# Second block of a two-block transformer kernel: GpSimd's arithmetic moved to VectorE, output projection in plain fp32, modulation sums moved

## The chip, the cores and the metric

The kernel runs on one core of a Trainium2 chip. TensorE (PE in the rows; PEld is its loading of weights), VectorE (DVE), ScalarE (ACT), GpSimd (POOL) and SyncE (SP, which only issues DMAs here) each work through their own list of instructions in order, and wait for each other by semaphores. The metric is the device time of one execution in microseconds (us), lower is better.

## The reference

The reference is two transformer blocks over 256 tokens of width 1024, in fp32. The first has attention (8 heads with a sliding window, 8 with forget gates) and a gated feed-forward part. The second block is what the change touches:

```python
mod = silu(c) @ w_ada + b_ada
sh_a, sc_a, g_a, sh_f, sc_f, g_f = split(mod, 6)
h = rmsnorm(x) * (1 + sc_a) + sh_a
qa, ka, va, q_lat, kv_lat, k_rope = split(h @ w_in)
o_a = windowed_gqa(qa, ka, va, sink)            # 8 heads, rotary, window 128
o_b = latent_attention(q_lat, kv_lat, k_rope)   # 8 heads, up-projections w_q_up, w_kv_up
mixed = concat([rmsnorm(o_a, g1), rmsnorm(o_b, g2)])
x = x + g_a * (mixed @ w_out)
h = rmsnorm(x) * (1 + sc_f) + sh_f
x = x + g_f * peer(h)                           # 16384 experts, 8 heads x 16 picks
```

It ends with a last norm of the rows. `peer` computes queries and scores, picks 16 experts a head, and in this kernel multiplies with all the rows of the two expert tables, `u` and `v`, 64 MB each.

## The kernel before

Tokens lie on the 128 partitions, in two tiles. A product in fp32 accuracy is made of three products of the type fp32r: both operands are split into a high part (a copy in fp32r) and a low part (the rest), and `mm3` (lines 141 to 145) adds high times high, high times low and low times high into one bank of PSUM. The operands of the two tiles of tokens stand split in `xh` and `xl`.

Weights come as units of 128 rows by up to 1024 columns. `plan` lists the units in the order of their use, `fetch` starts some, `unit` hands the next one out. `load` (lines 106 to 116) does three things for a unit: a DMA from SP's queue into one of three buffers `x`, a copy by ScalarE into one of four buffers `hi` (line 114), and a subtraction into one of four buffers `lo` (line 115). That subtraction is VectorE's work, but for the units that the list `POOLED` (line 38) names: all of `w_out_2` (output projection of the second block), seven of the eight of `w_swa` (its input projection for the windowed attention), `w_kvup` and both of `w_qup`. For those it is GpSimd's.

The stages around the change, in their order of time:

- The end of the feed-forward part (`ffn`, lines 960 to 1005): norms of two tiles of rows, the step to the operands of the second block (`scaled` transposes, `shifted` multiplies and adds, `split` makes `xh` and `xl`), and the products `lat_proj` with the weights `w_lat`. The low parts of the first tile's operands are GpSimd's work (line 604), those of the second VectorE's. VectorE and ScalarE keep the written order here (`in_order`).
- The input projection `swa_proj`, eight units with 12 products each, then `swa_rope`, which rotates queries and keys on VectorE (lines 1031 to 1036), `kv_up` and `q_up(0)`.
- The attention (`steps`, `attend`): eight pairs of heads, four of windowed attention (`swa`) and four of latent attention (`mla`). A pair goes through its stages one step behind the other: scores (line 410), maximum (414, 417 and 420), exponentials on ScalarE (427), division (447), transposes (465), product with the values (480), and the split of the outcome, times a gain, into `oh` and `ol` (491 and 494). A table of fills gives each step other work of TensorE, among it the output projection `wo`: pairs 0 and 1 in step 7, 2 and 3 in step 8, 4 in step 9.
- The tail (lines 1222 to 1257): products of pairs 5, 6 and 7, in TensorE's written order; `row_scale(sqb)`, the norm of the latent half; `post`, which scales a half of a tile, adds it to the rows (lines 536 and 537) and sums their squares; then the norm, the transposes and the operands of `peer`, whose query products come next. Two of the four additions of `post` and the first tile's low parts are GpSimd's.
- `ada_cols` makes 16 small products (line 229) that sum two of the six modulation vectors: 16 columns of them for shift 3 in step 1, for scale 4 in the tail.

Outside the stretches that `in_order` holds, a scheduler orders the instructions of each engine by the dependences of the written program.

## Time and profile before

| | |
|---|---|
| median of 3 runs | 1306.51 us (1304.98 to 1307.62) |
| the profiled execution, first to last instruction | 1306.6 us |
| TensorE busy | 1269.4 us, 97% |
| VectorE busy | 970.5 us, 74% |
| ScalarE busy | 684.5 us, 52% |
| GpSimd busy | 86.8 us, 7% |
| subtractions of weights on GpSimd (line 115) | 23, 50.9 us |
| share of the chain that ended last | PE 90%, DVE 7%, ACT 2%, DMA 1% |

The busy time of TensorE counts pipelined products whose ends are modelled, so the rate of a run of products is read from their starts. The granted clock (PEclk) is given as a share of 2.4 GHz: 1.00 is that level, 0.50 is 1.2 GHz, what lies between is a mixture over the stretch. GpSimd's share of the span is small, but nearly all of it lies between 318 and 464 us, the stretch from the end of the feed-forward part to the first query products of `peer`.

### The profile page before, as it was taken

What the parts mean: (1) busy time and instruction counts of PE and PEld (TensorE: products, weight loads), DVE (VectorE), ACT (ScalarE), POOL (GpSimd) and SP (SyncE); (2) the same over time, 40 slices, a digit from 0 to 9 for tenths busy, and PEclk for the clock granted to TensorE, in tenths of its full rate; (3) what the DMA queues carried; (4) which work ended last, traced back from release to release, by engine and by line L of the source; (5) the groups of instructions that cost most, each with busy time, mean ns of one, the idle gap of its engine ahead of it and who ended that gap; (6) DMA issues with size and microseconds to landing.
All of it is one profiled execution on the core that took longest, in us unless ns stands there. A gap on an engine that the chain in (4) does not pass through costs nothing.

```text
span 1306.6 us, 22860 instructions
## 1 busy us (share of the span) xinstructions
PE 1269.4 (97%) x8804; PEld 1160.8 (89%) x8804; DVE 970.5 (74%) x1908; ACT 684.5 (52%) x1241; POOL 86.8 (7%) x70
## 2 busy tenths in 40 slices
PE   8999999999888899999999999999999999999997
PEld 7887899999766699999999999999988888888886
DVE  5678878877777879989777889997555855555555
ACT  6655544454567455456555554445444554444543
POOL 2300100000351400000000000000000000000001
PEclk9999999999998989999999999999999999999999
DMA  6756588886241355555444444444576855555552
GB/s 216 217 188 216 184 289 292 285 281 226 62 135 31 116 191 169 186 169 192 158 135 146 146 145 145 139 149 167 186 253 208 296 195 186 193 177 193 190 185 93
DMA packets 67849, 239.50 MB, mean 183 GB/s; under 512 B 8499, under 2 KB 9155, under 8 KB 67452
## 3 DMA queue, kind: packets, MB, share of 16 engines
q1 hardware_dynamic: 66524, 233.53, 52.9%
q0 software_dynamic: 1216, 4.51, 1.1%
q8 instruction: 69, 1.13, 0.3%
q14 instruction: 40, 0.33, 0.1%
HBM read 235.87 MB, written 2.79 MB: 183 GB/s over the span
## 4 chain that ended last, share of the span: by engine, by line
PE 90%; DVE 7%; ACT 2%; DMA 1%; issue 1%; ACTq 0%; DVEq 0%
PE ps L143 24%; PE ps L144 23%; PE ps L145 23%; PE ps L345 3%; PE ps L348 3%; PE ps L347 3%; PE ps L1459 2%; PE ps L1460 2%; PE ps L410 1%; PE ps L465 1%; PE ps L480 1%; DVE lo L115 1%; PE ps L1486 1%; PE ps L229 0%; DVE h L537 0%
## 5 line engine op out<-in xcount | busy, mean ns | idle before, releaser
L114 ACT ACTIVATE hi<-x 128x1024 fp32r<-128x1024 f32 (+2 forms) x384 | 403.2, 1052 | 433.2 <-PE ps L145 181.6
L115 DVE TENSOR_TENSOR lo<-x,hi 128x1024 fp32r<-128x1024 f32 (+2 forms) x361 | 439.0, 1218 | 201.2 <-ACT hi L114 196.6
L143 PE MATMUL ps<-xh,hi 128*128 128x256 f32 (+2 forms) x1304 | 378.2, 290 | 1.4 <-ACT xh L573 1.0
L144 PE MATMUL ps<-xl,hi 128*128 128x256 f32 (+2 forms) x1304 | 368.5, 283 | 1.5 <-DVE xl L574 1.5
L145 PE MATMUL ps<-xh,lo 128*128 128x256 f32 (+2 forms) x1304 | 368.6, 283 | 0.0
L143 PEld LDWEIGHTS ps<-xh,hi 128*128 128x128 f32 (+1 forms) x1304 | 247.3, 190 | 3.2 <-ACT xh L573 1.2
L144 PEld LDWEIGHTS ps<-xl,hi 128*128 128x128 f32 (+1 forms) x1304 | 247.3, 190 | 2.7 <-POOL lo L115 1.7
L145 PEld LDWEIGHTS ps<-xh,lo 128*128 128x128 f32 (+1 forms) x1304 | 246.3, 189 | 0.6
L144 PE MATMUL ps<-lo,w 128*128 128x512 f32 (+1 forms) x640 | 223.3, 349 | 0.0
L143 PE MATMUL ps<-hi,w 128*128 128x512 f32 (+1 forms) x640 | 223.2, 349 | 0.0
L145 PE MATMUL ps<-hi,w 128*128 128x512 f32 (+1 forms) x640 | 221.9, 347 | 0.0
L143 PEld LDWEIGHTS ps<-hi,w 128*128 128x128 f32 x640 | 121.2, 189 | 16.9 <-ACT hi L114 0.2
L145 PEld LDWEIGHTS ps<-hi,w 128*128 128x128 f32 x640 | 120.8, 189 | 16.0
L144 PEld LDWEIGHTS ps<-lo,w 128*128 128x128 f32 x640 | 121.2, 189 | 15.4 <-issue 0.2
L345 PE MATMUL ps<-xh,hi 128*128 128x256 f32 x352 | 100.0, 285 | 0.6 <-ACT xh L573 0.6
L348 PE MATMUL ps<-xh,lo 128*128 128x256 f32 x352 | 98.7, 281 | 0.0
L347 PE MATMUL ps<-xl,hi 128*128 128x256 f32 x344 | 96.5, 281 | 0.0
L1469 DVE SCALAR_TENSOR_TENSOR W<-ps,W 128x160 f32<-128x160 f32 (+31 forms) x64 | 55.1, 865 | 31.0 <-ACT W L1508 30.2
L115 POOL TENSOR_TENSOR lo<-x,hi 128x1024 fp32r<-128x1024 f32 (+1 forms) x23 | 50.9, 2222 | 323.3 <-ACT hi L114 323.3
L345 PEld LDWEIGHTS ps<-xh,hi 128*128 128x128 f32 x352 | 66.2, 188 | 1.6 <-ACT xh L573 0.9
L348 PEld LDWEIGHTS ps<-xh,lo 128*128 128x128 f32 x352 | 66.3, 188 | 0.0
L347 PEld LDWEIGHTS ps<-xl,hi 128*128 128x128 f32 x344 | 65.1, 189 | 0.7
(346 smaller groups left out, 1706.2 us busy)
## 6 DMA issues: line engine op xcount, KB each, us to landing
x<-in_u SPq DMA_DIRECT2D x128, 512.0 KB, 3.5
x<-in_v SPq DMA_DIRECT2D x128, 512.0 KB, 3.5
x<-in_w_gu SPq DMA_DIRECT2D x44, 512.0 KB, 4.6
ada<-in_w_ada SPq DMA_DIRECT2D x40, 512.0 KB, 5.0
x<-in_w_down SPq DMA_DIRECT2D x22, 512.0 KB, 4.5
x<-in_w_in SPq DMA_DIRECT2D x18, 512.0 KB, 4.4
x<-in_w_out SPq DMA_DIRECT2D x16, 512.0 KB, 3.4
x<-in_w_query SPq DMA_DIRECT2D x16, 512.0 KB, 3.7
```

The lines of the kernel that those rows point to most:

```text
L114: nc.scalar.activation(hi[:, :w], x[:, :w], AF.Copy)
L115: low.tensor_sub(lo[:, :w], x[:, :w], hi[:, :w].bitcast(F32))
L143: mm(out, lhsT=lh, rhs=rh, start=start, stop=False)
L144: mm(out, lhsT=lh, rhs=rl, start=False, stop=False)
L145: mm(out, lhsT=ll, rhs=rh, start=False, stop=stop)
L345: mm(out, lhsT=wh[:, s], rhs=self.xh[:, k, :T], start=k == 0, stop=False)
L347: mm(out, lhsT=wh[:, s], rhs=self.xl[:, k, :T], start=False, stop=False)
L348: mm(out, lhsT=wl[:, s], rhs=self.xh[:, k, :T], start=False, stop=not apart and k == KT - 1)
L410: nc.tensor.matmul(S[tl, hd], lhsT=qT(tl, hd), rhs=kT(hd, n), start=True, stop=True)
L1459: nc.tensor.matmul(o, lhsT=bj[:, gq, :, q], rhs=ah[:, gq, :, q], start=True, stop=False)
L1460: nc.tensor.matmul(o, lhsT=bj[:, gq, :, q], rhs=al[:, gq, :, q], start=False, stop=True)
L1469: nc.vector.scalar_tensor_tensor(a, pv[:, :, :i0], 1.0 / GSC, a, op0=OP.mult, op1=OP.mult)
```

## The change

No arithmetic is left on GpSimd from the end of the feed-forward part to the end of the tail; it keeps one DMA there, which stores the rows. `POOLED` is gone, so the low parts of all split units are made by VectorE. The units of `w_out_2` are no longer split: `whole` loads them by DMA straight into rooms of the `hi` and `lo` buffers, by turns, as fp32. The outcome of a pair of heads is kept as one fp32 tile `o` instead of `oh` and `ol`, and `plain` multiplies it with the unit in fp32: four products for a pair, where there were twelve.

```diff
+WHOLE = ("w_out_2",)
-POOLED = [("w_out_2", c) for c in (0, 1, 2, 3, 4, 5, 6, 7)] + [("w_swa", c) for c in (0, 1, 2, 4, 5, 6, 7)] + [("w_kvup", None), ("w_qup", 0), ("w_qup", 1)]
...
+    def whole(self, name, i, w):
+        self.rooms = not self.rooms
+        n, b = (("lo", self.nl), ("hi", self.nh))[self.rooms]
+        x = self.strm.tile([128, 1024], F32R, name=self.nm("x"), tag=n, bufs=b).bitcast(F32)
+        self.nc.sync.dma_start(x[:, :w], self.t[name][i * 128:(i + 1) * 128])
+        return x
...
-        oh = w.tile([128, T], F32R, name=self.nm("oh"), tag="oh", bufs=6)
-        ol = w.tile([128, T], F32R, name=self.nm("ol"), tag="ol", bufs=6)
...
+            oh, ol = w.tile([128, T], F32, name=self.nm("o"), tag="o", bufs=8), None
             nc.scalar.activation(oh, O[:, :T], AF.Copy, scale=g)
...
-            nc.vector.scalar_tensor_tensor(ol, O[:, :T], g, oh.bitcast(F32), op0=OP.mult, op1=OP.subtract)
...
+    def plain(self, acc, c, o, w, start, stop, tiles=(0, 1)):
+        for tt in tiles:
+            for hf in range(2):
+                self.nc.tensor.matmul(acc[tt][hf], lhsT=o[:, tt * 128:(tt + 1) * 128], rhs=w[:, hf * 512:(hf + 1) * 512],
+                                      start=start, stop=stop)
```

In `ffn` the low parts of the first tile's operands go to VectorE, put off to a later place in its list, and the first three units of `w_swa` are fetched there, ahead of the second tile's operands (`plan` and `fetch` used to follow after `lat_proj`):

```diff
-            self.split(ym[0], 0, 0, (nc.gpsimd, nc.vector)[BX])
+            low = []
+            self.split(ym[0], 0, 0, nc.vector, low)
...
+            run(low)
             self.sum2(sr[:, 3:4], s2[1])
-            r = self.rstd(sr[:, 3:4], 1, D, lambda: self.split(ym[0], 0, 1, nc.gpsimd))
+            r = self.rstd(sr[:, 3:4], 1, D, lambda: self.split(ym[0], 0, 1, nc.vector, low))
             lat_proj(0, range(4))
             p1 = [self.scaled(xn[1], r, 1, hf) for hf in range(2)]
+            run(low)
             lat_proj(0, range(4, 8))
+            self.plan(*(("w_swa", i, 768) for i in range(8)))
+            self.fetch(3)
```

In the second block the sums for shift 3 move ahead of the attention, those for scale 4 from the tail into step 1. All eight units of `w_out_2` are fetched before the attention's first step, behind two units of `w_query`. Pairs 5 and 6 of the projection move from the tail into steps 9 and 10. In the tail the products of pair 7 for the second tile stand behind `row_scale`, and the four additions of `post` are VectorE's:

```diff
+        self.ada_cols(16, 3)
         swa_T(4)
         swa_T(0)
+        self.fetch(sum(s[0] == "w_out_2" for s in self.todo))
...
-            1: [do(swa_T, 2), do(self.ada_cols, 16, 3)] + ([do(q_up, 1)] if QL == 2 else []),
+            1: [do(swa_T, 2), do(self.ada_cols, 24, 4)] + ([do(q_up, 1)] if QL == 2 else []),
...
-            9: [fin, do(wo, 4)],
+            9: [fin, do(wo, 4), do(wo, 5)],
+            10: [do(wo, 6), lambda: self.fetch(2)],
...
-            for hf in range(2):
-                self.part(acc[4], items[:2], 0, hf)
+            self.plain(acc[4], 7, outs[7][0], last, False, True, (0,))
             rg = row_scale(sqb)
-            for part in (items[2:], 0), (items, 1):
-                for hf in range(2):
-                    self.part(acc[4], part[0], part[1], hf)
-            self.ada_cols(24, 4, late)
-            post(0, 0, nc.gpsimd)
-            post(0, 1)
-            post(1, 0, nc.gpsimd)
-            post(1, 1)
+            self.plain(acc[4], 7, outs[7][0], last, False, True, (1,))
+            for tt in range(2):
+                for hf in range(2):
+                    post(tt, hf)
...
-                self.split(ym[0], 0, hf, nc.gpsimd)
+                self.split(ym[0], 0, hf, nc.vector)
```

What the scheduler makes of it is seen at three places. The first is TensorE between `q_up(0)` and the first scores. Before (`qk` are the rotated queries and keys, `acc` the modulation sums, `hi` and `lo` of the weights `w_qup`):

```order
L143 MATMUL ps_4321<-hi_4270,lh 128x512
L144 MATMUL ps_4321<-lo_4271,lh 128x512
L145 MATMUL ps_4321<-hi_4270,ll 128x512
L1176 MATMUL ps_4344<-ident,qk 128x128
L1176 MATMUL ps_4348<-ident,qk 128x128 x2
```

And of the changed kernel, where line 238 is what 229 was, 1198 what 1176 was, and 151 to 153 are `mm3`:

```order
L151 MATMUL ps_4313<-hi_4270,lh 128x512
L238 MATMUL ps_4336<-ones,acc 128x128 x4
L238 MATMUL ps_4342<-ones,acc 128x128 x4
L1198 MATMUL ps_4348<-ident,qk 128x128 x2
L152 MATMUL ps_4314<-lo_4271,lh 128x256
L153 MATMUL ps_4314<-hi_4270,ll 128x256
L152 MATMUL ps_4313<-lo_4271,lh 128x512
L153 MATMUL ps_4313<-hi_4270,ll 128x512
L1198 MATMUL ps_4352<-ident,qk 128x128 x2
```

The sums have come in ahead of the transposes of `qk`, and four products of `q_up(0)` have moved behind the first pair of transposes: they use `lo_4271`, which VectorE now makes after its rotations.

The second is VectorE at the end of the feed-forward part of the changed kernel (`xl` and `ym` are the operands of the second block, 620 is the low part of a split, 115 that of weights):

```order
L596 TENSOR_SCALAR xn_3738<-h,s_3893 128x512
L620 TENSOR_TENSOR xl<-ym_3739,xh 128x4x128
L115 TENSOR_TENSOR lo_3941<-x_3939,hi_3940 128x768
L115 TENSOR_TENSOR lo_3947<-x_3945,hi_3946 128x768
L115 TENSOR_TENSOR lo_3953<-x_3951,hi_3952 128x768
L620 TENSOR_TENSOR xl<-ym_3740,xh 128x4x128
```

Three units of `w_swa` and one low part of operands stand where VectorE had nothing between `xn` and the low part of the second tile.

The third is TensorE at the end of the projection of the changed kernel (`o` is a pair's outcome, `x` a whole unit of `w_out_2`, 489 the product with the values of the last pair, 1177 `row_scale`, 559 the transposes for the operands of `peer`):

```order
L489 MATMUL ps_4887<-pt_4861,vm 64x256
L541 MATMUL ps_4875<-x_4364,o_4844 128x512
L541 MATMUL ps_4876<-x_4364,o_4844 128x512
L541 MATMUL ps_4877<-x_4364,o_4844 128x512
L541 MATMUL ps_4878<-x_4364,o_4844 128x512
L541 MATMUL ps_4875<-x_4366,o_4892 128x512
L541 MATMUL ps_4876<-x_4366,o_4892 128x512
L1177 MATMUL ps_4923<-ones,sqb 128x128 x2
L541 MATMUL ps_4877<-x_4366,o_4892 128x512
L541 MATMUL ps_4878<-x_4366,o_4892 128x512
L559 MATMUL ps_4971<-ident,xn 128x128 x4
```

Behind the last product with values stand 8 products in place of 36, and two of them follow `row_scale`, where 24 followed it.

## Rows read from the trace of the kernel before

**Rows 1.** Stretches of the span: busy time of each engine, PEclk, DMA.

```profile
349.00:373.50 24.50, 24.50 (x145) 21.55 (x143) 16.71 (x47) 16.36 (x30) 16.01 (x8) 1.00 0.43 136
373.50:397.00 23.50, 15.39 (x92) 11.32 (x90) 18.27 (x69) 14.52 (x46) 7.19 (x3) 0.83 0.27 89
415.00:448.00 33.00, 32.08 (x160) 23.80 (x159) 25.39 (x54) 16.49 (x39) 14.07 (x7) 1.00 0.25 80
448.00:464.00 16.00, 11.18 (x59) 10.14 (x58) 12.89 (x27) 9.99 (x20) 6.30 (x5) 0.68 0.34 121
```

**Rows 2.** TensorE's waits, 318 to 464 us: total us, times, longest.

```profile
PE ps L465 <- DVE sb L447: 5.7, 2, 3.9
```

**Rows 3.** Timeline of GpSimd beside line 420: start us, us, instruction.

```profile
386.41 4.71 POOL L115 TENSOR_TENSOR lo<-x,hi 128x1024 fp32r<-128x1024 f32 x2 [9.94 <-ACT hi L114]
388.94 2.21 DVE L420 TENSOR_SCALAR nm<-m 128x4 f32<-128x4 f32 x1
```

**Rows 4.** Timeline of VectorE, 333 to 336 us, norm of the second tile.

```profile
333.48 0.96 DVE L166 TENSOR_TENSOR s<-s 128x1 f32<-128x1 f32 x1
334.36 0.94 DVE L115 TENSOR_TENSOR lo<-x,hi 128x768 fp32r<-128x768 f32 x1
335.23 1.24 DVE L167 SCALAR_TENSOR_TENSOR s<-s,s 128x1 f32<-128x1 f32 x1
336.50 0.16 DVE L168 SCALAR_TENSOR_TENSOR s<-s,s 128x1 f32<-128x1 f32 x1
```

**Rows 5.** Timeline of VectorE, 368 to 377 us, the rotations.

```profile
368.26 1.53 DVE L1035 TENSOR_TENSOR qk<-qk,ra 128x256 f32<-128x256 f32 x1
369.72 0.41 DVE L1036 TENSOR_TENSOR qk<-qk,rb 128x256 f32<-128x256 f32 x1
370.58 1.89 DVE L1035 TENSOR_TENSOR qk<-qk,ra 128x64 f32<-128x64 f32 x1
372.40 0.21 DVE L1036 TENSOR_TENSOR qk<-qk,rb 128x64 f32<-128x64 f32 x1
374.19 2.56 DVE L1036 TENSOR_TENSOR qk<-qk,rb 128x256 f32<-128x256 f32 x1
```

**Rows 6.** Timeline of TensorE, 378 to 399 us, scores, sums and transposes.

```profile
378.69 2.01 PE L410 MATMUL ps<-kT,qT 64*128 64x256 f32 x8 [0.64 <-ACT qT L1178]
381.10 2.48 PE L229 MATMUL ps<-ones,acc 128*128 128x128 f32 x16
388.10 1.14 PE L410 MATMUL ps<-kT,qT 64*128 64x256 f32 x8
394.21 0.69 PE L465 MATMUL ps<-ident,sb 128*128 128x128 f32 x2 [3.95 <-DVE sb L447]
396.96 2.08 PE L410 MATMUL ps<-kT,qT 64*128 64x256 f32 x8
```

**Rows 7.** Timeline of TensorE: an fp32 product of 512 columns, and fp32r ones.

```profile
331.93 1.88 PE L248 MATMUL ps<-acc,ones 128*128 128x512 f32 x4
416.21 0.39 PE L143 MATMUL ps<-hi,oh 128*128 128x512 f32 x1
420.87 0.39 PE L145 MATMUL ps<-hi,ol 128*128 128x512 f32 x1
```

**Rows 8.** Timeline, 441 to 452 us, the tail.

```profile
441.79 0.68 PE L1155 MATMUL ps<-ones,sqb 128*128 128x128 f32 x4 [0.63 <-DVE sqb L496]
443.90 1.41 DVE L536 SCALAR_TENSOR_TENSOR tmp<-ps,s,ga 128x512 f32<-128x512 f32 x2
447.92 1.95 PE L229 MATMUL ps<-ones,acc 128*128 128x128 f32 x16
448.91 0.69 DVE L537 TENSOR_TENSOR h<-h,tmp 128x512 f32<-128x512 f32 x1
```

**Rows 9.** Groups by line of VectorE, 318 to 464 us: busy us, mean ns.

```profile
L494 DVE SCALAR_TENSOR_TENSOR ol<-ps,cols,oh 128x256 fp32r<-128x256 f32 x8 | 3.8, 475 | 0.9 <-ACT s L493 0.9
```

**Rows 10.** Line 580 by instruction, 318 to 464 us: ns min/median/max, first and last start.

```profile
L580 DVE TENSOR_SCALAR xn<-h,s x8: 473/479/2568, 330.1 to 455.1; 128x512 f32<-128x512 f32 x8
```

More of the change, by code (lines that the diff above doesn't have):

```diff
@@ L122, in fetch @@
             spec = self.todo.popleft()
-            self.loaded.append((spec[:2], self.load(*spec, low or (self.nc.gpsimd if spec[:2] in POOLED else self.nc.vector))))
+            self.loaded.append((spec[:2], self.whole(*spec) if spec[0] in WHOLE else self.load(*spec, low or self.nc.vector)))
             n -= 1
@@ L189, in setup @@
         self.nx, self.nh, self.nl = 3, 4, 4
+        self.rooms = False
         self.strm = self.ctx.enter_context(self.tc.tile_pool(name="strm", bufs=1, reuse_waits="tile"))
@@ L483, in attend @@
             nc.tensor.matmul(O[:, :T], lhsT=vmeta, rhs=ptm, start=False, stop=True, skip_group_check=True)
-        oh = w.tile([128, T], F32R, name=self.nm("oh"), tag="oh", bufs=6)
-        ol = w.tile([128, T], F32R, name=self.nm("ol"), tag="ol", bufs=6)
         if gain is None:
+            oh = w.tile([128, T], F32R, name=self.nm("oh"), tag="oh", bufs=6)
+            ol = w.tile([128, T], F32R, name=self.nm("ol"), tag="ol", bufs=6)
             nc.scalar.activation(oh, O[:, :T], AF.Copy)
@@ L599, in shifted, with split @@
             f()
-    def split(self, y, tt, hf, low):
+    def split(self, y, tt, hf, low, later=None):
         k, q = slice(hf * 4, hf * 4 + 4), slice(tt * 128, (tt + 1) * 128)
         self.nc.scalar.activation(self.xh[:, k, q], y[:, hf], AF.Copy)
-        low.tensor_sub(self.xl[:, k, q], y[:, hf], self.xh[:, k, q].bitcast(F32))
+        f = lambda: low.tensor_sub(self.xl[:, k, q], y[:, hf], self.xh[:, k, q].bitcast(F32))
+        return f() if later is None else later.append(f)
     def roots(self, x):
@@ L1048, in second_block @@
         nc.sync.dma_start(sink, t["swa_sink"].to_broadcast([128, 16]))
-        self.plan(*(("w_swa", i, 768) for i in range(8)), ("w_kvup", None, 1024), ("w_qup", 0, 768), ("w_qup", 1, 768),
+        self.plan(("w_kvup", None, 1024), ("w_qup", 0, 768), ("w_qup", 1, 768),
                   *(("w_out_2", c, 1024) for c in range(8)),
@@ L1185, in wo @@
                 acc[c] = self.accs()
-            self.out_proj(acc[c // 4 * 4], [(outs[c], self.unit("w_out_2", c), c % 4 == 0, c % 4 == 3)])
+            self.plain(acc[c // 4 * 4], c, outs[c][0], self.unit("w_out_2", c, False), c % 4 == 0, c % 4 == 3)
         ra = []
@@ L1218, in second_block @@
             8: [lambda: ra.append(row_scale(sqa)), do(wo, 2), do(wo, 3)],
-            9: [fin, do(wo, 4)],
-        })
-        items = [(outs[c], self.unit("w_out_2", c, False), False, c == 7) for c in (5, 6, 7)]
-        self.fetch(1, nc.gpsimd)
+            9: [fin, do(wo, 4), do(wo, 5)],
+            10: [do(wo, 6), lambda: self.fetch(2)],
+        })
+        last = self.unit("w_out_2", 7, False)
         xn = A.tile([128, 8, T], F32, name="xn", tag="qTm").rearrange("p (t a) b -> p t (a b)", t=2)
@@ L1229, in post @@
             self.h_squares(s2[tt], tt, hf)
[L1230 removed]
         with self.in_order(mybir.EngineType.PE):
[L1232 to L1233 removed]
+            self.plain(acc[4], 7, outs[7][0], last, False, True, (0,))
             rg = row_scale(sqb)
[L1235 removed]
+            self.plain(acc[4], 7, outs[7][0], last, False, True, (1,))
+            for tt in range(2):
                 for hf in range(2):
[L1237 to L1242 removed]
+                    post(tt, hf)
             for tt in range(2):
                 self.sum2(sr[:, tt:tt + 1], s2[tt])
[L1245 to L1247 removed]
+            r = self.rstd(sr, 2, D)
             p = {}
```

4 lines of the change are left out of this document (removed).

## The prediction

> **What bounds the kernel now.** I read the busy times of the engines by stretch first, since the whole span says little here: TensorE is busy 97% of it, and nothing of the change touches the long stretch of `peer` behind 464 us. Between the end of the feed-forward part and there it is another picture [rows 1]. From 349 to 373.5 us TensorE has no pause at all; from 373.5 to 397 it works 15.4 of 23.5 us, at a mean granted clock of 0.83; from 415 to 448, the output projection, it is busy again for 32.1 of 33.0; from 448 to 464 it works 11.2 of 16 at 0.68. So there are two stretches bound by products, and between and behind them chains in which VectorE and ScalarE pass work to each other and TensorE waits. The list of waits says for whom: most of all for the division of the softmax on VectorE, 5.7 us in two waits [rows 2].
>
> The timeline then shows why VectorE is late. GpSimd makes two low parts from 386.41 to 391.12; VectorE starts an instruction of 128x4 elements at 388.94, and it ends at 391.15, with GpSimd's work, after 2.21 us [rows 3], where instructions as small take 0.16 [rows 4]. The same is seen in the rotations, where one shape takes 0.41 and 2.56 us [rows 5], and in the step to the operands of `peer`, 0.48 and 2.57 [rows 10]. While GpSimd computes, some of VectorE's instructions stand still. That is what the change takes away. Against it stands work that goes to VectorE, and a dearer projection.
>
> **The change part by part.** The sum is made against the profiled execution's 1306.6 us; the median of the runs is 1306.51, so nothing to speak of lies around the span.
>
> *A, the end of the feed-forward part.* In the norm of the second tile two stalled instructions come back, 0.96 - 0.16 = 0.80 and 1.24 - 0.16 = 1.08, and between them a unit's low part of 0.94 leaves the chain [rows 4]: 2.82 us. In exchange three such low parts now stand ahead of the second tile's operands. VectorE was free there, so I let one of the three be in the way: 2.8 - 0.9 = 1.9. Bounds: 2.8 if all three find VectorE idle, and 2.8 - 3 x 0.94 = 0 if none does.
>
> *B, projection to first scores.* The rotations lose three stalls: 1.53 - 0.41, 1.89 - 0.21 and 2.56 - 0.41 [rows 5], together 4.95 us, and the first scores, at 378.69, wait for the rotations. What is late next? TensorE has no gap up to 373.5 [rows 1], and the 16 modulation sums, 1.95 us [rows 8], now stand in front of the first transposes. One low part, 0.94 us, stands on VectorE behind the rotations, and the products that need it lie between the two pairs of transposes. So 4.95 - 1.95 - 0.94 = 2.1. Bounds: 4.95 if both find room, 0 if in addition the moved subtractions of the other units take as much again.
>
> *C, the attention.* The stall of line 420 goes: 2.21 - 0.16 = 2.05 [rows 3, 4]; it lies on the way from scores to the wait of 3.9 us [rows 2]. TensorE runs twice at a lower clock there, near half (1.2 GHz). The first scores take 2.01 us and later ones of the same shape 1.14, the sums 2.48 against 1.95; after the long wait 12 transposes take from 394.21 to 396.96, and the scores behind them 2.08 [rows 6, 8]. With shorter waits I expect the clock to hold: 0.87 + 0.53 + (2.75 - 2.75/2) + 0.94 = 3.7. Each pair also loses one instruction of VectorE, the low part `ol`, 0.48 us [rows 9]. Two stood ahead of the division for which TensorE waits the second time, 5.7 - 3.9 = 1.8 us [rows 2]; I take 0.9. C = 2.05 + 3.7 + 0.9 = 6.6. Bounds: 2.9 if the clock falls as before, 6.6.
>
> *D, the price of fp32.* A pair costs 12 fp32r products before. From 416.21 to 420.87 there are 20 steps, 0.233 us each [rows 7], so 2.80 us a pair. A plain product of the same shape stands in line 248: two of them show as four passes in 1.88 us, which with the last one's modelled end of 0.16 (a single product shows 0.39 where the next one starts after 0.233) is 0.43 a pass and 0.86 a product. Four make 3.44, so 0.64 more a pair and 5.1 for eight. This stretch is TensorE's own [rows 1], so I count it whole. Bounds: 5.9 with 1.88 / 4 = 0.47 a pass; 4.2 if the 0.9 us that TensorE idles there are filled. What is gained before 415 us carries through, since TensorE then only starts earlier.
>
> *E, the tail.* Before, the projection ends at 447.92 and the last addition at 448.91 + 0.69 = 449.60: 1.7 us later, since three of four halves were scaled beside 24 products. Now two products follow `row_scale`. Its result reaches the first scaling 443.90 - 441.79 = 2.1 us after its start [rows 8]; it and the two products take 0.68 - 0.16 + 1.72 = 2.2 us of TensorE, so all four halves begin when TensorE ends. A half is 0.70 + 0.69 plus 0.06 between them: 5.8 us, 4.1 later than now. The moved sums, 1.95 us at 447.92, were hidden by this chain and cost nothing at either place in it. Behind it the stalled instruction of line 580 comes back, 2.57 - 0.48 = 2.1 [rows 10], as TensorE's transposes and all that follows wait for it. E = -4.1 + 2.1 = -2.0. Bounds: -4.1 to -1.
>
> Edits at no cost: ScalarE's eight copies of `w_out_2` go, but ScalarE is busy half of 415 to 448 [rows 1]. The raw units load from SP's queue behind two of `w_query`, and wait for rooms of the weights in front; the last rooms come free with `q_up(1)`, which ends before the scores at 388.10 [rows 6], 28 us before the first of these products [rows 7]. Queued behind them are further units of `w_query`, which are used in `peer` alone. The low parts of the operands of `peer`, now all on VectorE, run while TensorE works through the first halves.
>
> Sum: 1.9 + 2.1 + 6.6 - 5.1 - 2.0 = 3.5 us. 1306.6 - 3.5 = 1303.1.
>
> **The rivals.**
> *The clock falls as before.* TensorE ran slow behind the wait of 3.9 us [rows 2, 6], and the change leaves most of its other half, some 2 us, in place. Then C keeps 2.9 and the time is 1303.1 + 3.7 = 1306.8, no change. For it: the fall needs only one wait, and the tail's pause grows by 4 us. Against it: the waits in 373.5 to 397, the stretch with the lower clock [rows 1], lose most of their length by B and C.
> *VectorE becomes the bound (slower).* From 349 to 373.5 it is busy 16.7 us [rows 1]. Take away 4.95 of stalls and add eight low parts of 0.94, 7.5 us, and it has 19.3 of 24.5, in written order with a norm and rotations for which TensorE waits. If every one of the eight stands ahead of such work, TensorE waits 7.5 us that it does not wait now: 1303.1 + 7.5 = 1310.6. From 3.5 us on, half of them, nothing is left of the gain. The Trainium skill, Perfetto Trace Analysis, Optimizing Scalar/DVE Operations, says that when DVE is saturated it may help to give work to other engines, even GPSIMD, which is the change read backwards; it adds that both share a read port, so that moving work between them might not help. By the first half the time would be this rival's; the trace so far agrees with the second, since 2.21 us for an instruction of 0.16 is worse than doing the work oneself.
> *More comes back.* If the inserted sums and subtractions in A and B find gaps (+0.9 and +2.9), the gain is 7.3 and the time 1299.3. For it: a busy TensorE is not TensorE at its peak, so 349 to 373.5 may hold room. Against it: products are in order, and the sums come before the transposes.
>
> **How the numbers follow.** Forecast 0.45, with a range of its own of 1301 to 1305.5 from the bounds of D and E; clock as before 0.20 (1306.8); VectorE the bound 0.15 (1310.6); more comes back 0.20 (1299.3). A measurement of this kernel tells about 0.2%, 2.6 us: faster is below 1303.9, slower above 1309.1. Of the forecast I put four fifths below 1303.9: 0.36 + 0.20 = 0.56 faster, 0.09 + 0.20 = 0.29 same, 0.15 slower. The range for 8 in 10 goes from 1298.5, a little under the best rival, to 1309, where the slower one begins.
>
> **What would show it.** Right: line 420 and the rotations at 0.16 to 0.41 us throughout; first scores about 4 us earlier; PEclk near 1 from 373.5 to 397; the projection's products at 0.43 a pass without pauses, and its end only 2 to 6 us earlier; then some 8 us without products before the transposes. Wrong: TensorE's waits for `lo` of line 115 between 345 and 375 us, half the clock in the attention, or a granted clock below 0.68 in the 16 us around the first query products [rows 1].

## The result, and the profile after

| | before | changed |
|---|---|---|
| median of the runs | 1306.51 us (5 runs, 1304.98 to 1310.66) | 1300.85 us (5 runs, 1299.31 to 1302.17) |
| ratio | | 0.995, 95% interval 0.9934 to 0.9965 |
| profiled execution, span | 1306.6 us | 1299.1 us |

The change makes the kernel faster by 5.7 us in the medians and by 7.5 us between the two profiled spans. The run that was profiled with a span of 1299.1 us took 1300.85 us in all, and every profiled run of the experiments below shows the same 1.7 to 1.8 us around its span.

Two executions can be apart by 2 us before anything of the change begins (the clock of the first 25 us differs, see the last section), so I compare stages. The borders are starts on TensorE: the first transposes of `xn` at the end of the feed-forward part, the last eight products of `lat_proj` with `xl`, the first scores, the transposes of the fourth pair, the last product of the projection, the first query product. The five stages are the prediction's A to E. Of the kernel before, by stages (columns as in [rows 1]):

```profile
331.06:350.44 19.38, 14.58 (x70) 11.99 (x68) 13.95 (x31) 9.71 (x26) 6.04 (x4) 0.91 0.25 80
350.44:378.69 28.25, 24.09 (x142) 20.54 (x140) 20.63 (x56) 18.36 (x35) 18.50 (x9) 1.00 0.46 147
378.69:406.13 27.44, 21.76 (x129) 15.88 (x129) 21.26 (x88) 18.86 (x59) 4.71 (x2) 0.81 0.14 46
406.13:447.69 41.56, 40.64 (x216) 30.34 (x217) 33.38 (x78) 22.42 (x59) 13.76 (x7) 1.00 0.20 64
447.69:458.09 10.40, 5.60 (x34) 4.78 (x32) 7.68 (x20) 5.50 (x13) 5.33 (x4) 0.80 0.45 164
```

And of the changed kernel:

```profile
329.81:345.93 16.12, 13.56 (x70) 10.86 (x69) 14.44 (x36) 11.37 (x28) 0.00 (x0) 1.00 0.26 79
345.93:371.67 25.74, 25.22 (x157) 22.47 (x156) 19.80 (x71) 16.36 (x33) 0.00 (x0) 1.00 0.67 208
371.67:394.04 22.37, 19.39 (x128) 14.03 (x129) 16.85 (x80) 16.60 (x56) 0.00 (x0) 0.92 0.35 127
394.04:438.52 44.48, 44.34 (x183) 24.51 (x184) 25.45 (x69) 18.23 (x54) 0.00 (x0) 1.00 0.09 28
438.52:451.18 12.66, 4.27 (x19) 3.28 (x17) 10.45 (x26) 6.01 (x16) 0.58 (x1) 0.65 0.20 83
```

Three stages are shorter (3.26, 2.51 and 5.07 us), two are longer (2.92 and 2.26). Another 1.25 us lies before the first border, and 0.6 behind the last one. Of the 1.25, 0.13 is there already at 318.5 us, the same product on TensorE taken. The other 1.1 belongs to the change: GpSimd makes its first low part of `w_swa` from 319.25 to 321.1 us, and VectorE, late there by 0.95 us, takes 0.84 us for its instruction on `silu`, where it takes 0.42 in the changed kernel. Of the experiments below b2, which keeps GpSimd's part, has the 1.1 us too, and in b1, which takes it away, 0.2 is left. Of the kernel before (VectorE):

```profile
320.56 0.84 DVE L896 TENSOR_TENSOR silu<-y,silu 128x256 f32<-128x256 f32 x1 [0.54 <-ACT silu L895]
```

Of GpSimd's 86.8 us before, 51.7 lie between 318 and 464 us, so more than half and not nearly all of it; in the changed kernel its one DMA of 0.6 us is left there.

Where TensorE waits in the changed kernel, 318 to 464 us (total us, times, longest), answering [rows 2]:

```profile
PE ps L559 <- DVE xn L596: 8.0, 1, 8.0
PE ps L474 <- DVE sb L456: 3.0, 2, 1.9
PE ps L959 <- ACT xh L619: 2.6, 3, 1.1
```

The instructions of VectorE that stood still before, 310 to 464 us (ns min/median/max); line 429 answers to 420 in [rows 3], 1057 and 1058 to [rows 5], 596 to [rows 10]:

```profile
L429 DVE TENSOR_SCALAR nm<-m x8: 162/167/170, 374.5 to 413.4; 128x4 f32<-128x4 f32 x8
L1057 DVE TENSOR_TENSOR qk<-qk,ra x4: 222/324/426, 363.7 to 367.7; 128x256 f32<-128x256 f32 x2, 128x64 f32<-128x64 f32 x2
L1058 DVE TENSOR_TENSOR qk<-qk,rb x4: 225/326/427, 364.1 to 367.9; 128x256 f32<-128x256 f32 x2, 128x64 f32<-128x64 f32 x2
L596 DVE TENSOR_SCALAR xn<-h,s x8: 478/482/488, 328.6 to 447.7; 128x512 f32<-128x512 f32 x8
```

Every stall is gone: the maxima are what the free instructions took before. TensorE in the attention, answering [rows 6]:

```profile
371.67 1.14 PE L419 MATMUL ps<-kT,qT 64*128 64x256 f32 x8 [0.52 <-ACT qT L1200]
373.01 1.95 PE L238 MATMUL ps<-ones,acc 128*128 128x128 f32 x16
383.56 0.44 PE L474 MATMUL ps<-ident,sb 128*128 128x128 f32 x2 [1.95 <-DVE sb L456]
385.70 2.08 PE L419 MATMUL ps<-kT,qT 64*128 64x256 f32 x8
```

First scores and sums run at full clock now, and the long wait is 1.95 us in place of 3.95. But the third scores still take 2.08: half clock was granted once more behind that wait. The projection and the tail (TensorE and VectorE), answering [rows 7, 8]:

```profile
404.40 6.17 PE L541 MATMUL ps<-x,o 128*128 128x512 f32 x14
436.79 0.61 PE L1177 MATMUL ps<-ones,sqb 128*128 128x128 f32 x4
437.23 1.88 PE L541 MATMUL ps<-x,o 128*128 128x512 f32 x4
438.74 0.75 DVE L552 SCALAR_TENSOR_TENSOR tmp<-ps,s,ga 128x512 f32<-128x512 f32 x1
443.69 0.69 DVE L553 TENSOR_TENSOR h<-h,tmp 128x512 f32<-128x512 f32 x1
447.09 1.33 PE L559 MATMUL ps<-ident,xn 128*128 128x128 f32 x5 [7.97 <-DVE xn L596]
```

Fourteen passes (an fp32 product shows as two) start from 404.40 until the scores at 410.42: 0.43 a pass, as priced. In the tail all four halves begin when the products end, and TensorE waits 7.97 us.

### The profile page after: what moved, and what is told of

Same layout as the page of the kernel before. It is cut to its first block, busy times and chain, and to the rows that moved or that the text cites. A ratio compares the mean times of both kernels' runs of the same rounds, so it can differ in the third digit from the quotient of the medians.

```text
span 1299.1 us, 22747 instructions
## 1 busy us (share of the span) xinstructions
PE 1267.5 (98%) x8772; PEld 1151.2 (89%) x8772; DVE 960.4 (74%) x1918; ACT 676.1 (52%) x1233; POOL 35.6 (3%) x44
## 3 DMA queue, kind: packets, MB, share of 16 engines
q8 instruction: 69, 1.13, 0.3%
## 4 chain that ended last, share of the span: by engine, by line
PE 92%; DVE 4%; ACT 2%; DMA 1%; issue 0%; ACTq 0%; DVEq 0%
PE ps L151 24%; PE ps L152 23%; PE ps L153 23%; PE ps L354 3%; PE ps L357 3%; PE ps L356 3%; PE ps L1475 2%; PE ps L1476 2%; PE ps L541 2%; PE ps L419 1%; PE ps L474 1%; PE ps L489 1%; PE ps L238 1%; PE ps L1502 1%; DVE lo L115 0%
## 5 line engine op out<-in xcount | busy, mean ns | idle before, releaser
L114 ACT ACTIVATE hi<-x 128x1024 fp32r<-128x1024 f32 (+2 forms) x376 | 394.7, 1052 | 426.6 <-PE ps L153 174.7
L115 DVE TENSOR_TENSOR lo<-x,hi 128x1024 fp32r<-128x1024 f32 (+2 forms) x373 | 451.4, 1213 | 204.5 <-ACT hi L114 199.4
L1476 PE MATMUL ps<-al,bj 128*128 128x128 f16 x256 | 64.0, 297 | 0.0
```

What stands on the lines that cost most here:

```text
L114: nc.scalar.activation(hi[:, :w], x[:, :w], AF.Copy)
L115: low.tensor_sub(lo[:, :w], x[:, :w], hi[:, :w].bitcast(F32))
L1476: nc.tensor.matmul(o, lhsT=bj[:, gq, :, q], rhs=al[:, gq, :, q], start=False, stop=True)
```

## The experiments

Each was built from one of the two kernels and timed against the kernel before. Stage durations are by the same borders as above, in us, from each one's profiled execution, a single one; where two runs differ by 0.2 us or less I read no difference. In the diffs `...` stands for lines left out.

| kernel | ratio (95%) | A | B | C | D | E |
|---|---|---|---|---|---|---|
| before | 1 | 19.38 | 28.25 | 27.44 | 41.56 | 10.40 |
| changed | 0.9950 (0.9934 to 0.9965) | 16.12 | 25.74 | 22.37 | 44.48 | 12.66 |
| b1_low_vector | 0.9963 (0.9947 to 0.9980) | 20.14 | 24.29 | 29.86 | 40.81 | 10.40 |
| b2_plain_only | 0.9957 (0.9939 to 0.9975) | 19.33 | 24.69 | 21.37 | 44.56 | 11.14 |
| e1_low_gpsimd | 0.9956 (0.9939 to 0.9973) | 17.90 | 25.52 | 21.35 | 44.56 | 12.65 |
| e2_mm3 | 0.9939 (0.9915 to 0.9962) | 16.10 | 25.72 | 26.16 | 39.56 | 12.83 |
| e3_sums_back | 0.9935 (0.9912 to 0.9958) | 16.09 | 23.59 | 23.12 | 44.56 | 12.72 |
| e4_tail_order | 0.9904 (0.9881 to 0.9928) | 16.09 | 25.75 | 22.25 | 44.55 | 9.43 |
| e5_tail_sums | 0.9920 (0.9902 to 0.9939) | 16.11 | 23.59 | 24.12 | 44.48 | 8.85 |
| e6_tail_warm | 0.9918 (0.9898 to 0.9937) | 16.08 | 23.59 | 23.12 | 44.56 | 9.17 |
| f1_tail_filled | 0.9949 (0.9929 to 0.9969) | 16.12 | 23.59 | 24.68 | 44.56 | 11.40 |
| f4_ffn_undone | 0.9986 (0.9972 to 1.0000) | 19.71 | 25.75 | 22.37 | 44.49 | 12.66 |
| f5_mm3_last | 0.9932 (0.9912 to 0.9953) | 16.10 | 25.72 | 23.21 | 42.90 | 12.77 |
| f6_all | 0.9935 (0.9919 to 0.9952) | 16.11 | 23.59 | 24.99 | 43.69 | 9.47 |

What lies behind E is not in the table: from the first query product to the end the runs e3, e6, f1 and f5 take 846.1 to 846.2 us, all others 847.7 to 848.5. In the 6 us behind that border the granted clock was 1.00 in these four, and 0.60 in the changed kernel. As f5 has the same order of the tail as the changed kernel, these 1.7 us need no edit of the tail, and I count them for none.

**Low parts of weights back on GpSimd.** My theory was that stalls behind GpSimd's work were what the change removed; the rival, that VectorE's length was the limit.

```diff
+POOLED = [("w_swa", c) for c in (0, 1, 2, 4, 5, 6, 7)] + [("w_kvup", None), ("w_qup", 0), ("w_qup", 1)]
...
-... low or self.nc.vector)))
+... low or (self.nc.gpsimd if spec[:2] in POOLED else self.nc.vector))))
```

> The changed kernel, with the low parts of seven units of w_swa, of w_kvup and both units of w_qup back on GpSimd; w_out_2 stays whole and everything else as changed. If GpSimd's work makes VectorE's instructions stand still, and this was worth what the rows say: the norm of the second tile loses again 1 to 2.5 us (stalls of 0.80 and 1.08, against low parts of 0.94 that leave VectorE), the rotations lose 2.5 to 4.5 us (three stalls, 4.95 us, of which the two traces show 2.5 gained net), the attention little since its stalls came from w_out_2: 1304.5 to 1308 us, 0.3 to 0.55% slower than the changed kernel. If instead VectorE's length was the limit and GpSimd's help was worth having, these eight low parts of 0.95 us on VectorE cost up to 7.5 us and the time falls below 1300.8: 1294 to 1300. If neither matters and the gain came from w_out_2 alone: 1300.8 within 1 us.

Against the changed kernel only A is longer, by 1.8 us, and the ratio cannot be told from the changed kernel's. Of the three cases the last is nearest, and the trace says why: stalls come back, but hardly on the path. Timeline of GpSimd, VectorE and TensorE in this run (start us, us, instruction), at the end of the feed-forward part, in the rotations and in the attention:

```profile
339.66 6.03 POOL L116 TENSOR_TENSOR lo<-x,hi 128x768 fp32r<-128x768 f32 x3 [198.13 <-DVE xn L597]
339.89 2.33 DVE L621 TENSOR_TENSOR xl<-ym,xh 128x512 fp32r<-128x512 f32 x1
...
367.08 1.85 POOL L116 TENSOR_TENSOR lo<-x,hi 128x768 fp32r<-128x768 f32 x1 [0.84 <-ACT hi L115]
367.35 0.41 DVE L1057 TENSOR_TENSOR qk<-ps,rope 128x256 f32<-128x256 f32 x1
367.68 1.53 DVE L1058 TENSOR_TENSOR qk<-qk,ra 128x256 f32<-128x256 f32 x1
...
387.24 0.44 PE L475 MATMUL ps<-ident,sb 128*128 128x128 f32 x2 [1.94 <-DVE sb L457]
388.74 1.13 PE L420 MATMUL ps<-kT,qT 64*128 64x256 f32 x8
```

In the rotations one stall of 1.1 us is left of three, since the other two of [rows 5] had come from units of `w_out_2` (GpSimd's work at 369.72 and 373.99 us in the trace of before). The one left is hidden: B is not longer. C is 1.0 us shorter: the same wait, 1.94 us, and behind it scores of 1.13 in place of 2.08, so there the clock held.

**Before, with the projection changed alone.** If `w_out_2` is the point, this should give most of the gain.

```diff
+WHOLE = ("w_out_2",)
...
-            self.out_proj(acc[c // 4 * 4], [(outs[c], self.unit("w_out_2", c), c % 4 == 0, c % 4 == 3)])
+            self.plain(acc[c // 4 * 4], c, outs[c][0], self.unit("w_out_2", c), c % 4 == 0, c % 4 == 3)
```

> The kernel before, with nothing changed but the projection: w_out_2 loaded whole, one fp32 tile a pair, plain products in the old places and the old order of the tail; the other low parts stay on GpSimd, and so do its additions. The low parts of w_out_2 that fell into the rotations (369.72 and 373.99 us) and the scores (386.41) are gone, so if each stall costs what stands on the path: first scores 2 to 3.5 us earlier, the attention 3 to 5 us shorter, the projection 3 to 5 us longer by the price of fp32, the tail 0 to 2 us longer: ratio 0.996 to 1.000. If fp32's 5.1 us come whole and the clock falls as before: ratio 1.001 to 1.003.

Ratio 0.9957, within the interval of the whole change. B is 3.6 us shorter and C 6.1, D is 3.0 longer and E 0.7, and A stays. The other low parts and both additions are still GpSimd's here. The five stages add up to 121.1 us, 121.4 in the changed kernel and 127.0 before: what the rest of the change wins in A, it loses again in B, C and E, and the 1.1 us ahead of A are what is left of it.

**Before, with the low parts moved alone.**

```diff
-POOLED = [("w_out_2", c) for c in (0, 1, 2, 3, 4, 5, 6, 7)] + [("w_swa", c) ...] + [("w_kvup", None), ...]
+POOLED = []
```

> The kernel before, with nothing changed but the list of low parts: all of them on VectorE, also those of w_out_2, whose projection stays with three fp32r products. GpSimd keeps two additions and three low parts of operands. If the stalls are what the change gains from: the 23 low parts leave GpSimd, the norm of the second tile and the rotations get their stalls back (0.80, 1.08, and 1.11, 1.68, 2.14 us), first scores 3 to 5 us earlier; from there VectorE has 8 low parts of 1.22 us and 8 of 0.48 more than the changed kernel, which cost that kernel 5 us in the attention and gave 5 back in the projection (the run with three products): 1300 to 1304 us, ratio 0.995 to 0.998. If VectorE is too full for them (23 low parts, some 25 us, from 318 to 464): ratio 1.001 to 1.005.

The total is as expected, with the stages otherwise: B gains 4.0, C loses 2.4 and A 0.8. VectorE in the attention, and TensorE's wait:

```profile
388.31 1.19 DVE L115 TENSOR_TENSOR lo<-x,hi 128x1024 fp32r<-128x1024 f32 x1
389.43 0.60 DVE L447 TENSOR_SCALAR sb<-sb,den 128x256 f32<-128x256 f32 x2
389.82 1.59 PE L465 MATMUL ps<-ident,sb 128*128 128x128 f32 x6 [3.97 <-DVE sb L447]
```

Start us, us, instruction: the stall of line 420 is gone and TensorE still waits 3.97 us: a low part of `w_out_2` now stands in VectorE's list just ahead of the division. So C is not won by taking this work from GpSimd, but by not doing it at all.

**The changed kernel with three products.** The same from the other side.

```diff
-WHOLE = ("w_out_2",)
+WHOLE = ()
...
-                self.nc.tensor.matmul(acc[tt][hf], lhsT=o[:, tt * 128:(tt + 1) * 128], rhs=w[:, hf * 512:(hf + 1) * 512],
-                                      start=start, stop=stop)
+                self.mm3(acc[tt][hf], o[0][:, s], o[1][:, s], w[0][:, d], w[1][:, d], start, stop)
```

> The changed kernel with the projection in three fp32r products again: w_out_2 is split, ScalarE makes the high parts, VectorE the low parts and the low part of each pair; no arithmetic returns to GpSimd. If plain fp32 costs its 0.64 us a pair on the path, 5.1 us in all, and VectorE has the room (it is busy 11.8 of 18 and 19.7 of 33 us from 397 to 448): 3 to 5 us faster than the changed kernel, 1296 to 1298 us. If VectorE has not the room, since eight low parts of 1.22 and eight of 0.48 us, 13.6 us in all, come into its list between divisions and additions: no gain or slower, 1301 to 1306 us. My sum of before counted the price whole; from the two traces the stretch lost only 3.1 us, so between the two I expect about 1298.

The early fetch of all eight units is gone here too, and `o` is a pair of split tiles again. C loses 3.8 us and D wins 4.9; the total does not differ from the changed kernel's by more than the intervals. The list of waits of this kernel has the divisions again, twice as long as in the changed one:

```profile
PE ps L474 <- DVE sb L456: 6.1, 3, 2.7
```

The price of plain fp32 is 4.9 us, as priced (5.1), if nothing else disturbs the stretch.

**Three products for the last three pairs**, where VectorE has room.

```diff
-... self.whole(*spec) if spec[0] in WHOLE else ...
+... self.whole(*spec) if spec[0] in WHOLE and spec[1] < 5 else ...
...
-            7: [do(wo, 0), do(wo, 1)],
+            7: [do(wo, 0), do(wo, 1), lambda: self.fetch(3)],
```

> The changed kernel with three fp32r products for pairs 5, 6 and 7 alone; their units are split with VectorE's low parts, fetched in step 7, when the attention's scores are nearly done. The run with three products for all pairs lost 5 us in the attention, where VectorE was too full, and won 4.8 in the projection. Where VectorE has room (19.7 of 33 us busy from 415 on) the price comes back alone: three pairs by 0.54 us (3.49 less 2.95 a pair, counted from starts of products in both traces), 1.6 us, ratio 0.9935 to 0.9945. If the three low parts of 1.22 us and the low parts of the pairs delay divisions or row_scale: no gain or a loss, ratio 0.995 to 0.997.

D is 1.6 us shorter, as expected. C is 0.8 longer: TensorE waits 2.95 us for the division that it waited 1.95 for, since a low part of weights, 1.22 us, now stands at 379.05 us in VectorE's list just ahead of line 429. The ratio, 0.9932, cannot be told from 0.995 by the intervals.

**The end of the feed-forward part undone.**

```diff
-            self.split(ym[0], 0, 0, nc.vector, low)
+            self.split(ym[0], 0, 0, nc.gpsimd)
...
-            self.plan(*(("w_swa", i, 768) for i in range(8)))
-            self.fetch(3)
```

> The changed kernel without its part at the end of the feed-forward stage: the first tile's low parts on GpSimd at once, and the first units of w_swa fetched where they were. If that part gave what the two traces show there, 3.4 us from 322 to 349, of which two stalls (0.80 and 1.08 us) belong to low parts of weights that VectorE still makes here: the waits of TensorE at 335 to 342 come back by 2 to 3 us, ratio 0.9965 to 0.9975. If the low parts of the operands on GpSimd stall only what has room, or what is lost comes back behind it, because TensorE is busy with w_swa up to 369: no change against the changed kernel, ratio 0.995.

A goes back to 19.71, 3.6 us more, and nothing returns behind it. Another 0.7 us is lost between 318 us and the first border, where a low part of `w_swa` now stands on VectorE ahead of `silu`. The ratio, 0.9986, is 4.7 us above the changed kernel's. VectorE and GpSimd in the norm of the second tile, and TensorE behind it:

```profile
331.31 0.95 DVE L115 TENSOR_TENSOR lo<-x,hi 128x768 fp32r<-128x768 f32 x1
333.00 0.94 DVE L115 TENSOR_TENSOR lo<-x,hi 128x768 fp32r<-128x768 f32 x1
333.81 1.30 POOL L620 TENSOR_TENSOR xl<-ym,xh 128x512 fp32r<-128x512 f32 x1 [195.35 <-ACT xh L619]
333.87 1.25 DVE L175 SCALAR_TENSOR_TENSOR s<-s,s 128x1 f32<-128x1 f32 x1
339.24 1.75 PE L959 MATMUL ps<-lat,xh 128*128 128x416 f32 x4 [2.96 <-ACT xh L619]
```

With two low parts and a stall of 1.1 us, the chain from line 578 to the end of line 176 takes 4.1 us, where it takes 1.5 in the changed kernel, and TensorE waits 2.96 us behind it, in place of 0.51. On either engine the low parts of `w_swa` are in the way if fetched there; the change puts them behind the norm.

**The sums where they were.**

```diff
-        self.ada_cols(16, 3)
         swa_T(4)
...
-            1: [do(swa_T, 2), do(self.ada_cols, 24, 4)] ...
+            1: [do(swa_T, 2), do(self.ada_cols, 16, 3)] ...
...
+            self.ada_cols(24, 4, late)
```

> The changed kernel with the modulation sums where they were: shift 3 in step 1 of the attention, scale 4 in the tail behind the projection. The first transposes then no longer wait behind 16 sums: the rotations end at 368.1 in the trace of the changed kernel and the first transposes start at 369.62, so about 1.5 us come back there, and in the tail the 1.95 us lie in an 8 us wait and cost nothing but two small additions on VectorE, at most 0.5 us: 1299.3 to 1300, 1.0 to 1.5 us faster. If the sums also keep TensorE's clock up in the tail, 0.5 to 1 us more. If products behind the transposes wait for their low part of weights anyway (VectorE makes it from 368.00 to 368.96), or the moved sums were hidden: 1300.8, no change.

The first transposes and scores of this run on TensorE:

```profile
367.33 0.82 PE L1198 MATMUL ps<-ident,qk 128*128 128x128 f32 x6
369.02 0.70 PE L419 MATMUL ps<-kT,qT 64*128 64x256 f32 x2 [0.87 <-ACT kT L1202]
```

B is 2.2 us shorter. C gives 0.8 of it back, E does not change: the sums fit into the tail's wait. By the stages this part of the change cost 1.4 us; the two ratios cannot be told apart.

**The order of the last products**, by tiles, with `row_scale` ahead of six of them in place of two.

```diff
-            10: [do(wo, 6), lambda: self.fetch(2)],
+            10: [lambda: self.fetch(2)],
...
-            self.plain(acc[4], 7, outs[7][0], last, False, True, (0,))
+            self.plain(acc[4], 6, outs[6][0], w6, False, False, (0,))
             rg = row_scale(sqb)
+            self.plain(acc[4], 7, outs[7][0], last, False, True, (0,))
+            self.plain(acc[4], 6, outs[6][0], w6, False, False, (1,))
             self.plain(acc[4], 7, outs[7][0], last, False, True, (1,))
```

> The changed kernel with another order of the last products: pairs 6 and 7 by tiles, pair 6 tile 0, then row_scale, pair 7 tile 0, pair 6 tile 1, pair 7 tile 1. If the tail is VectorE's chain of four halves, which starts when row_scale's result is there and the half is summed: that result comes 2.1 us after row_scale, which now starts at about 433.3 in place of 436.8, so tile 0's two halves, 2.8 us, run beside the last 3.4 us of products, and the four halves end about 441.5 to 442 in place of 444.3: 2 to 2.9 us faster, 1298 to 1299. If the tail is bound by the end of the products and not by VectorE's halves, or a longer wait lowers the clock of the query products: no change, 1300.8.

`row_scale`, the first scaled half and the transposes (TensorE and VectorE):

```profile
431.87 0.61 PE L1177 MATMUL ps<-ones,sqb 128*128 128x128 f32 x4
433.91 0.75 DVE L552 SCALAR_TENSOR_TENSOR tmp<-ps,s,ga 128x512 f32<-128x512 f32 x1
442.38 3.68 PE L559 MATMUL ps<-ident,xn 128*128 128x128 f32 x16 [4.75 <-DVE xn L596]
```

VectorE scales the first half 2.0 us after `row_scale` and beside the products; TensorE waits 4.75 us in place of 7.97, and E is 3.2 shorter. This version beats both kernels: 1296.18 us, ratio 0.9904, its interval apart from the changed kernel's. Of the 4.7 us between its span and the changed kernel's 3.3 lie in the stages and 1.4 ahead of them, where the clock of the first 25 us was 1.00 in place of 0.91.

**Both, and products of no use in the tail** (16 in the second run, against none in the first).

```diff
             self.plain(acc[4], 7, outs[7][0], last, False, True, (1,))
+            late = []
+            self.ada_cols(24, 4, late)
+            self.warm(16)
```

> The changed kernel with both: the last products by tiles with row_scale ahead, and the modulation sums where they were (shift 3 in step 1, scale 4 behind the last product). By the traces of the two alone, the sums gave 2.3 us at the first transposes and 2.7 in the end, the order of the tail 4.7; if they add up: 7 us under the changed kernel, ratio 0.988 to 0.990, 1291 to 1294 us. If the shorter tail no longer hides the sums, 1.95 us, or the first scores' gain is lost in the attention: ratio 0.990 to 0.992.

> The run with both, and 16 products of no use behind the sums in the tail, about 1.8 us at full clock, in what is left of the wait for the transposes. In the run with the new order of the tail, TensorE idled 4.7 us and ran at half clock from 441.04 to 451.28, which makes the 16 transposes 3.67 us and the first query products 0.21 each in place of 0.12. If activity ahead of the transposes holds the clock: 2 to 4 us less than the run without them, ratio 0.985 to 0.988. If the clock falls all the same, since some pause stays: no change against it. If the added products hold up the transposes: up to 1 us more.

The two did not add up: the ratio is 0.992, where 0.988 to 0.990 was expected. B keeps the sums' 2.2 us, but against the run with the new order alone C gives back 1.9 in the first run and 0.9 in the second, where the clock held. With the new order the sums alone were enough for full clock up to the first query product: the transposes take 1.94 us without the added products and 1.91 with them, in place of 3.68. In both runs TensorE then waits 1.47 us for the first operands, in place of 0.41 in the run with the new order alone. The added products take 3.6 us, not 1.8, and make E 0.3 longer. The second run's span was the shortest of all, 1291.3, but 1.4 of its 3.6 us under the first run's lie ahead of the first border and 1.5 behind the last; in the ratios the two are alike.

**Both sums in step 1, and more products of no use.**

```diff
-            1: [do(swa_T, 2), do(self.ada_cols, 24, 4)] ...
+            1: [do(swa_T, 2), do(self.ada_cols, 16, 3), do(self.ada_cols, 24, 4)] ...
...
             self.plain(acc[4], 7, outs[7][0], last, False, True, (1,))
+            self.warm(34)
```

> The changed kernel with the last products by tiles and row_scale ahead, the sums for shift 3 and those for scale 4 both in step 1 of the attention, and 34 products of no use, 3.8 us, in the wait for the transposes in the tail. By the three runs on the tail: the order gives 4.7 us, the clock of the transposes and first query products 2 to 3, the sums out of the way of the first transposes 1.5, and with no sums in the tail their two small additions do not hold up the first operands (in the two runs with sums there TensorE waited 1.47 us for them, in the one without 0.41): 1290 to 1294 us, ratio 0.985 to 0.989, the fastest so far. If the two groups of sums in step 1 only move the 1.95 us into the attention, or the added products hold up the transposes: ratio 0.990 to 0.992.

TensorE in the tail:

```profile
438.23 7.75 PE L147 MATMUL ps<-ones 128*128 128x128 f32 x68
```

My own size was wrong: each of the 34 products is two passes, 68 in the row, 7.6 us in place of 3.8, and the transposes stand behind them, at 445.82. VectorE had begun `xn` at 442.59. Ratio 0.9949.

**All that had paid, together**: the edits of the run with 16 products of no use and those of the three products for the last pairs.

> The changed kernel with what paid in the runs so far: last products by tiles with row_scale ahead, sums where they were, 16 products of no use in the tail, and three fp32r products for pairs 5, 6 and 7. If the terms add up, the run with the first three (profiled at 1291.3 us) loses another 1.6 to 1.8 us in the projection: 1289.5 us profiled, ratio 0.988 to 0.990. If the price of fp32 hid part of VectorE's halves in the tail, so that fewer products there only lengthen its wait (the two tiles' halves run beside the last products, 5.1 us of them in plain fp32): no gain against that run, ratio 0.991 to 0.992.

The terms did not add up: D gained 0.9 of 1.6, `row_scale` waited 0.60 us, and C was 1.9 longer than in the run with 16 products of no use. Of this 0.9 is left against the first of the two runs with both (24.12), where the clock fell in C as it did here. Ratio 0.9935. The order of the tail alone keeps the lowest ratio, though its interval overlaps those of the two runs with both.

## Why the prediction was right, and where it was not

Forecast 1303.1, measured 1300.85: faster, inside the range for 8 in 10, and 2.3 us lower, just under the forecast's own range (1301 to 1305.5). The gain came from the places named, but A was sized too small, the price of D too high and the clock's share of C too large, and the base was wrong too. That these errors partly cancelled is luck.

**The base.** "Nothing to speak of lies around the span" failed: 1.7 to 1.8 us lie there in every run that shows both. The profiled execution of before, span 1306.6, would then have taken about 1308.3, 1.8 above the median. That this span is as long as the median run was a coincidence. Span to span I forecast 3.5 us and 7.5 came; of the medians, 5.7.

| step | predicted | stage measured | what failed |
|---|---|---|---|
| A | +1.9 | +3.3, and +1.1 ahead of it | size |
| B | +2.1 | +2.5 | little |
| C | +6.6 | +5.1 | the clock |
| D | -5.1 | -2.9 | "TensorE's own" |
| E | -2.0 | -2.3, and +0.6 behind it | nothing |

*A.* The norm gave 2.5 of the 2.82 us [rows 4], as TensorE's wait for it shows, before and in the changed kernel:

```profile
340.58 1.21 PE L942 MATMUL ps<-lat,xh 128*128 128x416 f32 x4 [3.05 <-ACT xh L603]
336.71 1.03 PE L959 MATMUL ps<-lat,xh 128*128 128x416 f32 x4 [0.51 <-ACT xh L619]
```

For the 0.94 that I charged, TensorE waits 1.1 us ahead of the second tile's operands. Not priced were the 1.1 us ahead of the border, a third stall (line 580 at 340.82 us, 1.42 in place of 0.48) and about 1.0 us of half clock: the granted clock of the stage was 0.91 before, 1.00 after. The undone run shows that it is not GpSimd's weights alone: with none of their low parts on GpSimd, two of them in the chain on VectorE, the stalls behind the operands' split and the lower clock (0.91 again) cost 3.6 us.

*B.* The sums cost their 1.95 (2.2 by the run without them). But the 4.95 us of stalls were not all on the path: the run with low parts back on GpSimd has one of them, and its B is not longer.

*C.* The wait lost 2.0 us, as priced by line 420's stall, and the second wait 0.7 of 0.9. Of the clock's 3.7 some 2.0 came: scores 0.87, sums 0.53, and 12 transposes from 2.75 to 2.14 us, 0.6 of 1.37; the 0.94 of the next scores did not, since half clock was granted there again. The reason was too narrow, though: b1 and e2 show that without the stall, but with the low parts on VectorE, C is 3.8 to 7.5 us longer than here. What the change wins there it wins by not splitting `w_out_2`; b2, which changes nothing else, has it all.

*D.* The pass cost 0.43 and the price, in stretches free of GpSimd, 4.9. The sentence "this stretch is TensorE's own, so I count it whole" failed. Before, D held 2.0 us that three products need not cost (41.56 against 39.56 in e2): counting starts, about 0.9 us each is lost ahead of `row_scale`, whose input came late (0.63 of it idle, [rows 8]), and at the products with values, behind a VectorE of which three additions (line 537) took 1.7 to 2.9 us in place of 0.69. These went with GpSimd's work. Also, a pair cost more than my 2.80: the 96 products took 23.56 us of starts without that idle time, 2.95 a pair, since the first behind other work starts its successor 0.32 later, not 0.233. And my upper bound was a slip: 0.47 a pass is 3.76 a pair, which makes 7.7 us and not 5.9.

*E.* Chain and stall were as priced: the four halves take 5.6 us (5.8), the wait 7.97 (8).

Of the rivals, more coming back (1299.3) was nearer than the forecast, 1.6 us against 2.3, but for another reason than named: the sums found no gap. The clock did fall once; in e1 and b2, where it did not, C is 1.0 shorter. VectorE as the bound was real in the attention, wherever the low parts of `w_out_2` were put on it; in B, where I looked for it, seven low parts came to VectorE and not eight, as one of GpSimd's eight there [rows 1] was of `w_out_2`. Of the signs I named, the line 429, the pass of 0.43 and 7.97 us without products came; the first scores were 7.0 us earlier in place of 4, the projection's end 9.2 in place of 2 to 6, and the attention held 0.92 of the clock, not 1. Of the signs against me one came: in the 16 us around the first query product (441.09 to 457.09) the granted clock was 0.57, under the 0.68 of before. It was a poor sign, since from that product on the kernel is 0.6 us faster than before, not slower.

## What to carry to other kernels

A stall that the trace shows is worth what waits behind it: give each its own follower before adding them up, since here the one stall left in the rotations cost nothing, and ten low parts put back on GpSimd cost 1.8 us, all of it in the feed-forward part. Splitting work that moves from one engine to another can keep its price; ask what happens if it is not done at all, and buy that with the engine that has a stretch of its own. Compare by stages between markers, not by totals, where two executions differ by as much as a change does, and check what lies around the span before adding to it.

## What the hardware showed

**Which instructions stand still.** In the fence of the first experiment, a rotation that reads a bank of PSUM (`ps`) ran in 0.41 us beside GpSimd, and the next, of the same shape with both operands in SBUF, took 1.53 and ended 0.28 us behind GpSimd's work. Counted over the traces of before, b1, b2 and e1, from 300 to 470 us: of 72 instructions of VectorE that began under an arithmetic instruction of GpSimd and read PSUM, none was longer than the same instruction without it, by over 0.1 us; of 61 that read no PSUM, 44 were. Of the other 17, six began less than 0.07 us before GpSimd's end, and eleven were small ones with one tile to read or none. The Trainium skill, SBUF — State Buffer, Who interferes with whom, has this rule: two inputs in SBUF contend with a GpSimd instruction that reads SBUF, and so does a two-port mode; at most one SBUF input outside such a mode does not; and the shared ports are an exclusive lock. The traces agree, with 2.21 us for 0.16 as the largest ratio.

**The clock after a wait.** The same wait in the attention was followed by half clock in the changed kernel (1.95 us, then scores of 2.08) and by full clock in e1 and b2 (1.94 and 1.95 us, scores of 1.13). What decided between the two is open: no run here was made for it. In the first 25 us the clock differs between executions too, which moves all that follows. From 5 to 25 us, the changed kernel:

```profile
5.00:25.00 20.00, 16.43 (x121) 14.13 (x121) 12.81 (x35) 10.52 (x19) 4.91 (x3) 0.91 0.66 222
```

and the run with low parts on GpSimd, where nothing differs in that stretch, and the work behind it starts 2.2 us later:

```profile
5.00:25.00 20.00, 15.50 (x102) 13.13 (x102) 12.19 (x33) 8.47 (x17) 4.90 (x3) 0.83 0.62 211
```

**The first product of a run is dearer.** Behind transposes, sums or products with values in fp32, the first fp32r product of 512 columns starts its successor 0.31 to 0.34 us later, where 0.233 is usual. That the change of kind is the cause is not shown; no run separates it from the change of shape. TensorE's timeline of the run with three products for the last pairs, from a product with values on:

```profile
429.67 1.09 PE L489 MATMUL ps<-pt,vm 128*64 128x256 f32 x8
430.69 0.50 PE L151 MATMUL ps<-hi,oh 128*128 128x512 f32 x1
431.03 0.40 PE L152 MATMUL ps<-lo,oh 128*128 128x512 f32 x1
431.26 0.39 PE L153 MATMUL ps<-hi,ol 128*128 128x512 f32 x1
```

0.34 from the first start to the second, then 0.23. Plain fp32 among the other fp32 work of the attention pays little of this: the 64 passes take 0.434 on average, 0.43 in the run of fourteen.
